# Square sums on GpSimd, norm operations among the residuals, and filter spectra dealt behind two channel tiles

## The chip, the cores and the metric

The kernel runs on one core of a Trainium2 chip. TensorE (PE) multiplies, VectorE (DVE) and ScalarE (ACT) work elementwise, GpSimd (POOL) is a third, slower elementwise engine that also issues some DMAs, and SyncE (SP) issues most of them. Each engine works through its own queue in order; semaphores tie them together. SBUF is the on-chip memory, PSUM the memory into which TensorE accumulates and from which VectorE and ScalarE read. The metric is the time of one execution in microseconds (us), here the median of the runs.

## The reference

A two-layer encoder on a sequence of 1024 vectors of 1024 features. Layer 0 mixes by attention, layer 1 by a Hyena operator; each is followed by a convolutional feed-forward network (FFN). What this case touches:

```python
x = x + g2 * conv_ffn(h, ffn_w_up[i], ffn_conv_w[i], ffn_conv_b[i], ffn_w_down[i])   # layer 0, end
h = rmsnorm(x, norm1_g[i]) * (1.0 + sc1) + sh1                                       # layer 1, start

def hyena_mixer(h, ...):
    u = dwconv3(h @ w_in, conv_w, conv_b)          # 1024 -> 3072 channels, 3-tap convolution in time
    v, x1, x2 = jnp.split(u, 3, axis=-1)
    ...                                            # filt: two filters from a small network
    kf = jnp.fft.rfft(k2, axis=0)                  # the filter spectra
    gates = (x1, x2)
    zc = v
    for o in range(HY_ORDER):
        zf = jnp.fft.rfft(zc.astype(jnp.float32), n=2 * L, axis=1)
        y = jnp.fft.irfft(zf * kf[None, :, o], n=2 * L, axis=1)[:, :L]
        zc = gates[o] * (y.astype(h.dtype) + skip[o] * zc)
    return zc @ w_out
```

The norm divides each time step by the root of the mean of its squares over all 1024 features, so no output of it exists before the last feature tile of `x` is done. The spectra of the filters do not depend on `x`.

## The kernel before

Activations lie feature-major: 8 tiles of 128 features x 1024 time steps, worked on in two halves of 512 time steps (`HS`). Every matrix product is made of three matmuls on operands that are split into a high and a low part: high x high, low x high, high x low. One matmul multiplies a 128x128 weight block by 128x512 of the activations.

**The seam.** The last part of layer 0's FFN (`ffn(0, ...)`, which calls `seam`, L241) runs in an order written out by hand for TensorE, VectorE and ScalarE. For each half, eight steps: TensorE accumulates a feature tile in `d_ps` (L1296); VectorE adds it to the residual stream (`xd`, `res`, L980); ScalarE squares the new `xd` (`sq`, L981); VectorE adds the square to the running sum `ssq` (L268; the first square is the sum's start and the last is left to TensorE). Then `rstd_sums` (L230, L231) sums `ssq` and the last square over the partitions by 16 tiny matmuls with a column of ones, ScalarE takes the root (L232), VectorE the reciprocal (L233), and `rstd_spread` (L237) puts it on all partitions in a PSUM tile called `nrm`. `norm_ops` (L306) then lists 16 operations of VectorE per half: a scale (L314, `tt<-xd,acol,nrm`) and a low part (L318, `fh_l<-tt,mod,fh_h`) for each of the eight feature tiles; the high part between them (L315, `fh_h`) is ScalarE's. The dictionary `plan` says how many of the first half's 16 operations are run behind each step of the second half; before, it is empty, and four (`MID`) are run behind the last step. The others run as the matmuls of the next stage need them.

**The opening of the Hyena layer.** `w_in` has 24 channel tiles of 128 channels, 48 matmuls of 128x512 each (24 per half). Channel tiles 0 and 1 start inside the seam with their first half (`w_in_half`, `gemm_h`, L358). Then `w_in_stream` (L1382) yields after every matmul, so that others can be put between: the second half of channel tiles 0 and 1, channel tile 2 with a PSUM buffer of its own (pool `y1`), and then the others with a ring of two PSUM buffers (`pst`, which tiles 0 and 1 also use). Behind each channel tile, `dwconv` convolves in time: ScalarE starts `u` from the PSUM tile (L363) and VectorE adds the two other taps (L364, L365); the PSUM buffer is free when the last of them is done. Four transposes each (`u_tr`, L1389) turn half of a `u` into time-major form, which ScalarE copies to `gs` (L1391). The tuple `TRM` and the pair (10, 22) say ahead of which matmul of a channel tile such a group stands.

**Filter spectra.** `Filt` (L542) has eight units. Each loads the time-domain filter (`eo<-ed`, L557, 1 MB for each of two parts); the first load waits for a copy from the last low parts of the norm into the buffer (L556). `dif` makes sums and differences on VectorE (`pm`, `u`, `t`, `hf`, `ge`, `ri`, L372, L375), and TensorE multiplies them by a table (`f_ps`, L578 and following). While the units run, `MM_RATE` deals matmuls of `w_in_stream` among them by an account of VectorE's and TensorE's time. `MM_PRE` is the number of matmuls drawn ahead of it; before, 1 + 0, where the one draw runs the whole opening up to the end of channel tile 2.

**The conv stage** multiplies the spectra and transforms back (`z_ps` L1551, `ab_ps` L1573, `prod` L1643); the matmuls of `w_in` that are left are dealt among its steps by `rate` (L1751).

Outside the blocks written out by hand a scheduler orders the instructions by priorities (`HP` raises one); in the blocks from the spectra on only TensorE's order is by hand.

## Time and profile before

| | |
|---|---|
| Three runs | 2951.65, 2956.84, 2960.39 us; median 2956.84 |
| Profiled execution | 2955.43 us, its span 2953.7, mean granted clock 0.986 |
| TensorE busy | 2820.9 us (96%) |
| VectorE busy | 2326.6 us (79%) |
| ScalarE busy | 1237.2 us (42%) |
| GpSimd busy | 324.6 us (11%) |
| Seam and opening | from about 1434.7 to 1515.8 us of the span |
| Filter spectra | 1515.8 to about 1815 |
| Conv stage with matmuls of `w_in` | about 1815 to 1994 |

Rows of a timeline give the start and the length in us, the engine, the line of the kernel, the operation, the tile written and those read, the shape, and how many like instructions are put together; in brackets stands how long the engine had been idle before, and what it had waited for. Rows of windows give for each stretch the busy time and number of instructions of each engine, TensorE's granted clock (1.00 is full), the busy share of the DMA engines, and GB/s. Rows of waits give the total, the number and the longest wait.

### The profile page before, as it was taken

Reading aid. Unit: us, or ns where it says so; the run is one execution under the profiler, and the core shown is the slowest. Engines: PE = TensorE matmul, PEld = TensorE weight load, DVE = VectorE, ACT = ScalarE, POOL = GpSimd, SP = SyncE. Lnnn points to the kernel's source line nnn. Section 1 sums busy time; section 2 is a strip of 40 time slices with the busy share of each in tenths; the row PEclk is TensorE's granted clock in tenths of the full one; section 3 lists DMA queues with packets and bytes.
Section 4 is the critical chain, followed back from the end, with each engine's and each line's share of the span. In section 5 each row is a group of like instructions: output and inputs, shape, how many; then the busy total and the mean of one; then the engine's idle time right before and its main releaser. Section 6 shows DMA issues by size and latency. Waiting matters only on the chain.

```text
span 2953.7 us, 36529 instructions
## 1 busy us (share of the span) xinstructions
PE 2820.9 (96%) x13152; PEld 2301.5 (78%) x13152; DVE 2326.6 (79%) x3221; ACT 1237.2 (42%) x2004; POOL 324.6 (11%) x356
## 2 busy tenths in 40 slices
PE   5989999999999999999999999999988999999998
PEld 4777777778888887888777877877767788887887
DVE  8787989869988887877767885888867887777544
ACT  3557888843544443343432332223233433333211
POOL 0064564400011001111000000000000000000000
PEclk9999999999999999999999999999999999999999
DMA  7262222145455555665455665555754332224321
GB/s 276 92 185 66 54 76 51 50 169 190 139 187 182 177 174 176 207 184 156 140 199 190 225 206 197 174 173 184 245 195 153 123 104 87 86 79 143 122 86 57
DMA packets 221400, 440.02 MB, mean 149 GB/s; under 512 B 22210, under 2 KB 117218, under 8 KB 216740
## 3 DMA queue, kind: packets, MB, share of 16 engines
q1 hardware_dynamic: 184292, 391.54, 39.7%
q0 software_dynamic: 36928, 46.15, 5.7%
q8 instruction: 104, 1.70, 0.2%
q14 instruction: 76, 0.62, 0.1%
HBM read 308.62 MB, written 128.99 MB: 148 GB/s over the span
## 4 chain that ended last, share of the span: by engine, by line
PE 63%; DVE 9%; DMA 4%; issue 1%; ACT 1%; SPq 0%; DVEq 0%; ACTq 0%; POOLq 0%
PE w_ps L1063 26%; PE d_ps L183 14%; PE u_ps L1437 5%; PE d_ps L1296 2%; PE wo_y L183 2%; PE ab_ps L1573 2%; PE f_ps L183 2%; PE g_ps L358 2%; PE f_ps L578 1%; PE v_ps L358 1%; PE f_ps L579 1%; DVE prod L1643 1%; PE wo_y L1036 1%; DMA y<-yd 1%; DMA rd<-fw 1%
## 5 line engine op out<-in xcount | busy, mean ns | idle before, releaser
L1155 ACT CAST w_hi<-u 128x1024 fp32r<-128x1024 f32 x120 | 125.8, 1049 | 234.6 <-PE w_ps L1063 221.9
L162 DVE TENSOR_TENSOR pT_lo<-pt_ps,pT_hi 128x512 fp32r<-128x512 f32 x256 | 167.8, 681 | 46.7 <-ACT pT_hi L859 44.9
L1261 DVE SCALAR_TENSOR_TENSOR xd<-d_ps,mod,xd 128x1024 f32<-128x1024 f32 x104 | 132.7, 1280 | 76.5 <-PE d_ps L183 76.4
L1063 PE MATMUL w_ps<-t_h,w_hi 128*128 128x512 f32 x480 | 190.6, 397 | 1.9 <-ACT w_hi L1155 1.9
L1063 PE MATMUL w_ps<-t_h,w_lo 128*128 128x512 f32 x480 | 189.9, 397 | 0.4 <-DVE w_lo L162 0.4
L1063 PE MATMUL w_ps<-t_l,w_hi 128*128 128x512 f32 x480 | 190.0, 396 | 0.0
L162 DVE TENSOR_TENSOR w_lo<-u,w_hi 128x1024 fp32r<-128x1024 f32 x120 | 146.6, 1223 | 54.4 <-ACT w_hi L1155 54.2
L859 ACT CAST pT_hi<-pt_ps 128x512 fp32r<-128x512 f32 x256 | 145.1, 588 | 69.5 <-PE pt_ps L854 63.7
L183 PE MATMUL d_ps<-s_hi,wd_lo 128*128 128x512 f32 x544 | 170.0, 391 | 0.0
L183 PE MATMUL d_ps<-s_lo,wd_hi 128*128 128x512 f32 x544 | 169.9, 391 | 0.0
L183 PE MATMUL d_ps<-s_hi,wd_hi 128*128 128x512 f32 x544 | 168.9, 390 | 0.0
L838 DVE TENSOR_REDUCE nmx<-s_ps 128x1 f32<-128x1024 f32 x128 | 155.5, 1217 | 12.8 <-PE s_ps L831 10.9
L854 PE MATMUL pt_ps<-ident,p_t 128*128 128x128 f32 x1024 | 154.4, 274 | 10.0 <-DVE pT_lo L162 9.0
L854 PEld LDWEIGHTS pt_ps<-ident,p_t 128*128 128x128 f32 x1024 | 126.5, 141 | 44.8 <-DVE pT_lo L162 8.0
L848 ACT ACTIVATE p_t<-s_ps,nmx 128x1024 f32<-128x1024 f32 x128 | 143.7, 1124 | 3.5 <-DVE nmx L838 2.3
L1437 PE MATMUL u_ps<-fh_h,w_lo 128*128 128x512 f32 x368 | 132.3, 418 | 2.4 <-DMA w_lo<-wld 2.4
L1573 PE MATMUL ab_ps<-prod,dfti 128*128 128x256 f32 x512 | 124.2, 386 | 7.7 <-DVE prod L1643 2.4
L1437 PE MATMUL u_ps<-fh_l,w_hi 128*128 128x512 f32 x368 | 127.5, 413 | 0.0
L1063 PE MATMUL w_ps<-fh_h,w_hi 128*128 128x512 f32 x320 | 124.9, 390 | 0.7 <-ACT w_hi L1155 0.7
L1063 PE MATMUL w_ps<-fh_l,w_hi 128*128 128x512 f32 x320 | 124.8, 390 | 0.0
L1063 PE MATMUL w_ps<-gh_h,w_hi 128*128 128x512 f32 x320 | 124.7, 390 | 0.0
L1063 PE MATMUL w_ps<-gh_l,w_hi 128*128 128x512 f32 x320 | 124.7, 390 | 0.0
(424 smaller groups left out, 7568.4 us busy)
## 6 DMA issues: line engine op xcount, KB each, us to landing
u<-in_w_up_dram SPq DMA_DIRECT2D x80, 512.0 KB
w_raw<-in_w_down_dram SPq DMA_DIRECT2D x44, 512.0 KB
sg<-gate SPq DMA_DIRECT2D x40, 512.0 KB
w_raw<-sg SPq DMA_DIRECT2D x40, 512.0 KB
w_raw<-in_ada_w_dram SPq DMA_DIRECT2D x32, 512.0 KB
ed<-eo SPq DMA_DIRECT2D x64, 256.0 KB
eo<-ed SPq DMA_DIRECT2D x16, 1024.0 KB
kd<-k_sb SPq DMA_DIRECT2D x64, 256.0 KB
```

The source lines that it names most:

```text
L162: V.tensor_tensor(lo, src, hi.bitcast(F32), op=SUB)
L183: mm(out[:, cs], lhsT=a, rhs=b[:, cs], start=start and i == 0, stop=stop and i == 2)
L358: mm(pp[:, HS[hf]], lhsT=(wh, wh, wl)[i][:, ks], rhs=hd[hf][i % 2][k], start=k == 0 and i == 0, stop=k == n - 1 and i == 2)
L838: V.tensor_reduce(nmx, s_t[u, i], op=ALU.max, axis=AX.X, negate=True)
L848: nc.scalar.activation(p_t, s_ps, AF.Exp, bias=nmx, accum_out=sums[u][:, i:i + 1])
L854: nc.tensor.transpose(tp[:, i * P:(i + 1) * P], pts[u, i][:, sb * P:(sb + 1) * P], ident)
L859: nc.scalar.copy(ph, pt_t[u, sb][0])
L1063: mm(out, lhsT=(w[0], w[0], w[1])[i][:, k * P:(k + 1) * P], rhs=b[i % 2][k], start=k == 0 and i == 0, stop=k == 3 and i == 2)
L1155: nc.scalar.copy(w[0], src)
L1261: ins = V.scalar_tensor_tensor(x[dt_], yp, gate[dt_], x[dt_], op0=MUL, op1=ADD)
L1437: mm(yp[:, HS[hf]], lhsT=(wh, wh, wl)[i][:, k * P:(k + 1) * P], rhs=hd[hf][i % 2][k], start=k == 0 and i == 0, stop=k == KT - 1 and i == 2)
L1573: mm(ap[:, i], lhsT=dfti[:, m, :], rhs=v, start=n == 0, stop=n == len(ops) - 1)
```

## The change

Two things change in the seam of layer 0, three in the opening. (1) `plan` is {3: 1, 4: 1, 5: 1, 6: 1}: one norm operation of the first half behind each of the steps 3 to 6 of the second. (2) The six adds of squares of the second half are GpSimd's. (3) The opening block holds channel tiles 0 and 1 alone; channel tile 2 is streamed like those behind it, takes its buffer from the ring of two, and the pool `y1` is gone. (4) `MM_PRE` is 60: 48 matmuls of the block and 12 of channel tile 2 are drawn in the hand order ahead of the first unit of the spectra, and the dealing begins there. (5) Channel tile 2 has transposes ahead of its matmuls 18, 26, 38 and 46 instead of 10, 22, 40 and 47. The number of matmuls in `rate` follows from it. The lines of the changed kernel lie by one higher in the seam.

```diff
@@ -26,11 +26,12 @@
 NFFT = 2 * L
 LAGS = 2
 TRM = (40, 47)
+TR2 = (18, 26, 38, 46)
 NZ = 10
 ZC = 0.3
 TC_DELAY = 4
 TC_SPACE = 0
-MM_PRE = 0
+MM_PRE = 60
 PP = 300
 EK = ((0, 7), (1, 3))
 TC0 = 3
@@ -238,7 +239,7 @@
 
     MID = 4
 
-    def seam(n, step, result, ops, tps, at, plan, nxt=(), lows=()):
+    def seam(n, step, result, ops, tps, at, plan, nxt=(), lows=(), adders=(V, V)):
         todo = []
 
         def run(k):
@@ -265,7 +266,7 @@
 
             def later():
                 if not first and i < n - 1:
-                    V.tensor_tensor(ssq[:, cs], ssq[:, cs], sq, op=ADD)
+                    adders[hf].tensor_tensor(ssq[:, cs], ssq[:, cs], sq, op=ADD)
             return later, sq
 
         with tc.manual_schedule(engines={mybir.EngineType.PE, mybir.EngineType.DVE, mybir.EngineType.Activation}):
@@ -1299,7 +1300,8 @@
         def result(hf, dt_):
             return res(yps[hf, dt_], x[dt_], gate[dt_], HS[hf], dt_ == 0, sq_tile(sqp))
 
-        seam(KT, step, result, lambda hf, yt: ops(hf, tp_, yt), tps, ((12, 20), at), plan, nxt() if nxt else ())
+        seam(KT, step, result, lambda hf, yt: ops(hf, tp_, yt), tps, ((12, 20), at), plan, nxt() if nxt else (),
+             adders=(V, V if l else nc.gpsimd))
         tail_end(tps, False)
         sqp.release()
         (sb if l else wdt).release()
@@ -1355,7 +1357,7 @@
             yield from gemm_h(w_in2, hd, True, range(1))
         return go()
 
-    ffn(0, "left", "right", pre, ops0, {}, (0, 6), w_in_half, l1_work)
+    ffn(0, "left", "right", pre, ops0, {3: 1, 4: 1, 5: 1, 6: 1}, (0, 6), w_in_half, l1_work)
 
 
     up = [tc.alloc_tile_pool(name="hy_u", bufs=1)]
@@ -1364,7 +1366,6 @@
     dftf = dftp.tile([P, NFW + 6, P], F32, name="dftf")
     nc.sync.dma_start(dftf, t["dft_f"])
     fpool = tc.alloc_tile_pool(name="flt", bufs=1, side="right")
-    y1 = tc.alloc_tile_pool(name="y1", bufs=1, space=PSUM)
     F = Filt(fpool, "f", dftf)
     units = [(o, c4) for c4 in range(4) for o in range(2)]
     vdifs, f_done, seen = [], [], set()
@@ -1380,7 +1381,7 @@
             yield c, 0
 
     def w_in_stream():
-        pend, gs, gbufs, first, nw = [], None, 2, [], 0
+        pend, gbufs, nw = [], 2, 2
 
         def channels_to_time(u, gs, ct, hf):
             part, c4 = ct // 8, ct % 8 // 2
@@ -1406,38 +1407,30 @@
                 dwconv(yp, [col(C_HW + 24 * i + c_) for i in range(3)], col(C_HB + c_), u)
             pend.extend(lambda hf=hf: channels_to_time(u, gs, c_, hf) for hf in range(2))
 
-        for ct in [2 * p_ + i for p_ in (0, 1, 2, 3, 4, 5, 8, 9, 6, 7, 10, 11) for i in range(2)]:
+        gs = new_gs()
+        for k in range(KT):
+            for (wh, wl), yp in w_in2:
+                for i in range(3):
+                    mm(yp[:, HS[1]], lhsT=(wh, wh, wl)[i][:, k * P:(k + 1) * P], rhs=hd[1][i % 2][k],
+                       start=k == 0 and i == 0, stop=k == KT - 1 and i == 2)
+                    yield
+        for c_ in range(2):
+            conv(c_, w_in2[c_][1], gs)
+        for ct in [2 * p_ + i for p_ in (1, 2, 3, 4, 5, 8, 9, 6, 7, 10, 11) for i in range(2)]:
             with tc.high_priority(HP):
                 nw += 1
-                if ct < 2:
-                    first.append(w_in2[ct])
-                    continue
                 if nw % 3 or f_done:
                     wh, wl = wt.load(t["w_in"][ct], wld[ct])
                 else:
                     wh, wl = load_split(t["w_in"][ct], fpool, 1, lo_src=wld[ct])
-            if ct < 3:
-                first.append(((wh, wl), y1.tile([P, L], F32, name="u_ps", tag="y")))
-                order = [(hf, k, c_, i) for hf, cs in ((1, (0, 1)), (0, (2,)), (1, (2,))) for k in range(KT)
-                         for c_ in cs for i in range(3)]
-            else:
-                yp = pst("u_ps")
-                order = [(hf, k, 3, i) for k in range(KT) for i in range(3) for hf in range(2)]
-            for m, (hf, k, c_, i) in enumerate(order):
-                if c_ < 3:
-                    (wh, wl), yp = first[c_]
-                    m -= 48
-                    if m == 0:
-                        for c_ in range(2):
-                            if c_ == 0:
-                                gs = new_gs()
-                            conv(c_, first[c_][1], gs)
-                if pend and m in (TRM if ct > 3 else (10, 22) + TRM):
+            yp = pst("u_ps")
+            order = [(hf, k, i) for k in range(KT) for i in range(3) for hf in range(2)]
+            for m, (hf, k, i) in enumerate(order):
+                if pend and m in (TRM if ct > 2 else TR2):
                     pend.pop(0)()
                 mm(yp[:, HS[hf]], lhsT=(wh, wh, wl)[i][:, k * P:(k + 1) * P], rhs=hd[hf][i % 2][k],
                    start=k == 0 and i == 0, stop=k == KT - 1 and i == 2)
-                if ct > 2:
-                    yield
+                yield
             if ct % 2 == 0:
                 if f_done and gbufs == 2:
                     up.pop().release()
@@ -1447,8 +1440,6 @@
                 assert len(vdifs) < 2
                 gs = new_gs()
             conv(ct, yp, gs)
-            if ct == 2:
-                yield
         for f in pend:
             for _ in range(FLUSH):
                 yield
@@ -1463,11 +1454,10 @@
             yield v
 
     gemm = counted(w_in_stream())
-    for _ in range(1 + MM_PRE):
-        next(gemm)
-    y1.release()
     F.ps = f_ps = tc.alloc_tile_pool(name="flt_ps", bufs=3, space=PSUM, side="right")
     with tc.manual_schedule(engines={mybir.EngineType.PE}):
+        for _ in range(MM_PRE):
+            next(gemm)
         owed = 0.0
         for dve, pe in F.run(units, vdifs):
             owed += (MM_RATE * dve - pe) / 0.16
@@ -1748,7 +1738,7 @@
     n_tc = n_wo = 0
     with tc.manual_schedule(engines={mybir.EngineType.PE}):
         w = sum(max(c - MM_CBASE, MM_CMIN) for n in range(G_END) for c in step_cost(n))
-        rate = (1 + 21 * 48 + 2 * FLUSH - n_mm[0]) / w
+        rate = (48 + 22 * 48 + 2 * FLUSH - n_mm[0]) / w
         for n, c in conv_steps(JOBS, on_done):
             if gemm:
                 owed += rate * max(c - MM_CBASE, MM_CMIN)
```

VectorE at the end of the seam, from the fifth residual of the second half to the reciprocal (`xd_1086n` is feature tile n of the residual stream, `fh_l` a low part, `tt` a scaled tile). Before:

```order
L980 SCALAR_TENSOR_TENSOR xd_10864<-d_ps,mod,xd_10864 128x512
L268 TENSOR_TENSOR ssq<-ssq,sq 128x512
L980 SCALAR_TENSOR_TENSOR xd_10865<-d_ps,mod,xd_10865 128x512
L268 TENSOR_TENSOR ssq<-ssq,sq 128x512
L980 SCALAR_TENSOR_TENSOR xd_10866<-d_ps,mod,xd_10866 128x512
L268 TENSOR_TENSOR ssq<-ssq,sq 128x512
L980 SCALAR_TENSOR_TENSOR xd_10867<-d_ps,mod,xd_10867 128x512
L268 TENSOR_TENSOR ssq<-ssq,sq 128x512
L314 SCALAR_TENSOR_TENSOR tt<-xd_10860,acol,nrm 128x512
L314 SCALAR_TENSOR_TENSOR tt<-xd_10861,acol,nrm 128x512
L314 SCALAR_TENSOR_TENSOR tt<-xd_10862,acol,nrm 128x512
L318 SCALAR_TENSOR_TENSOR fh_l_13380<-tt,mod,fh_h_13372 128x512
```

VectorE at the same place in the changed kernel:

```order
L315 SCALAR_TENSOR_TENSOR tt<-xd_10860,acol,nrm 128x512
L981 SCALAR_TENSOR_TENSOR xd_10864<-d_ps,mod,xd_10864 128x512
L315 SCALAR_TENSOR_TENSOR tt<-xd_10861,acol,nrm 128x512
L981 SCALAR_TENSOR_TENSOR xd_10865<-d_ps,mod,xd_10865 128x512
L315 SCALAR_TENSOR_TENSOR tt<-xd_10862,acol,nrm 128x512
L981 SCALAR_TENSOR_TENSOR xd_10866<-d_ps,mod,xd_10866 128x512
L319 SCALAR_TENSOR_TENSOR fh_l_13380<-tt,mod,fh_h_13372 128x512
L981 SCALAR_TENSOR_TENSOR xd_10867<-d_ps,mod,xd_10867 128x512
L315 SCALAR_TENSOR_TENSOR tt<-xd_10863,acol,nrm 128x512
L319 SCALAR_TENSOR_TENSOR fh_l_13381<-tt,mod,fh_h_13373 128x512
L315 SCALAR_TENSOR_TENSOR tt<-xd_10864,acol,nrm 128x512
L319 SCALAR_TENSOR_TENSOR fh_l_13382<-tt,mod,fh_h_13374 128x512
```

The adds are gone from VectorE; three scales and a low part stand between the residuals instead, and eight operations of the first half are ahead of the second half's reciprocal where four were.

VectorE behind the norm, from the last low part on (`pm`, the numbered `u` and `t`, `hf`, `ge` belong to the first spectra unit; `u<-u_ps,cols,u` are the taps of channel tiles 0 and 1). Before:

```order
L318 SCALAR_TENSOR_TENSOR fh_l_13406<-tt,mod,fh_h_13398 128x512
L556 COPY eo<-fh_l_13387 1x1
L556 COPY eo<-fh_l_13402 1x1
L364 SCALAR_TENSOR_TENSOR u<-u_ps,cols,u 128x1023
L372 TENSOR_TENSOR pm<-eo 128x1024
L372 TENSOR_TENSOR pm<-eo 128x768
L372 TENSOR_TENSOR pm<-eo 128x256
L364 SCALAR_TENSOR_TENSOR u<-u_ps,cols,u 128x1023
L365 SCALAR_TENSOR_TENSOR u<-u_ps,cols,u 128x1023
L372 TENSOR_TENSOR u_13951<-pm 128x256 x2
L372 TENSOR_TENSOR t_13949<-pm 128x2x256 x2
```

VectorE at the same place in the changed kernel, from the first `pm` on:

```order
L373 TENSOR_TENSOR pm<-eo 128x1024
L373 TENSOR_TENSOR pm<-eo 128x768
L373 TENSOR_TENSOR pm<-eo 128x256
L373 TENSOR_TENSOR u_13882<-pm 128x256 x2
L365 SCALAR_TENSOR_TENSOR u<-u_ps,cols,u 128x1023
L373 TENSOR_TENSOR t_13880<-pm 128x2x256 x2
L376 SCALAR_TENSOR_TENSOR hf<-pm 128x512
L376 SCALAR_TENSOR_TENSOR ge<-pm,eo 128x512 x2
L365 SCALAR_TENSOR_TENSOR u<-u_ps,cols,u 128x1023
L366 SCALAR_TENSOR_TENSOR u<-u_ps,cols,u 128x1023
```

The operations of the spectra now stand ahead of the taps; the last row, the second tap of channel tile 0, is the thirteenth instruction behind `eo`.

TensorE at the border between the two opening channel tiles and channel tile 2, with the semaphores of its waits (DMAHW and DMASW are loads). Before:

```order
L1437 MATMUL u_ps<-fh_l_13406,w_hi 128x512
L1437 MATMUL u_ps<-fh_h_13398,w_lo 128x512
L1437 MATMUL u_ps<-fh_h_13372,w_hi 128x512 [waits DMAHW3_49,DMAHW4_49,DMAHW2_49,DMAHW5_49,DMAHW1_49,DMAHW6_49,DMAHW0_49,DMAHW7_49,PE_49,Activation_49]
L1437 MATMUL u_ps<-fh_l_13380,w_hi 128x512
L1437 MATMUL u_ps<-fh_h_13372,w_lo 128x512 [waits DMASW2_49]
L1437 MATMUL u_ps<-fh_h_13373,w_hi 128x512
```

TensorE there in the changed kernel:

```order
L1414 MATMUL u_ps<-fh_l_13406,w_hi 128x512
L1414 MATMUL u_ps<-fh_h_13398,w_lo 128x512
L1431 MATMUL u_ps<-fh_h_13372,w_hi 128x512 [waits DMAHW3_49,DMAHW4_49,DMAHW2_49,DMAHW5_49,DMAHW1_49,DMAHW6_49,DMAHW0_49,DMAHW7_49,DVE_49,Activation_49]
L1431 MATMUL u_ps<-fh_h_13391,w_hi 128x512
L1431 MATMUL u_ps<-fh_l_13380,w_hi 128x512
L1431 MATMUL u_ps<-fh_l_13399,w_hi 128x512
L1431 MATMUL u_ps<-fh_h_13372,w_lo 128x512 [waits DMASW2_49]
```

The first matmul of channel tile 2 (on `fh_h_13372`) now waits for VectorE too: for the second tap of channel tile 0, whose buffer it takes. Over the whole of TensorE's order, 134 matmuls of `u_ps` stand ahead of the first of `f_ps` where 170 did (with 2 groups of `u_tr` instead of 6), 700 among the spectra in both, 40 between the spectra and `z_ps`, and 278 in the conv stage where 242 did.

## The prediction, made before the result was known

> **What bounds the kernel now.** I read first the busy shares, then the windows around the seam (end of the first FFN, norm, opening of the Hyena layer), then TensorE's and VectorE's timelines there.
>
> ```profile
> PE 2820.9 (96%) x13152; PEld 2301.5 (78%) x13152; DVE 2326.6 (79%) x3221; ACT 1237.2 (42%) x2004; POOL 324.6 (11%) x356
> ```
>
> TensorE sets the end: it is idle for 133 us of the span of 2953.7. A change can pay only where TensorE is idle or at a low clock. The windows (span, busy time of PE, PEld, DVE, ACT, POOL, granted clock, DMA share, GB/s):
>
> ```profile
> 1463.00:1476.80 13.80, 13.80 (x51) 11.17 (x51) 13.41 (x22) 7.32 (x11) 0.00 (x0) 0.78 0.13 54
> 1488.50:1491.00 2.50, 0.09 (x2) 0.03 (x1) 1.37 (x2) 2.19 (x2) 0.49 (x1) 1.00 1.03 416
> 1502.00:1515.80 13.80, 10.60 (x50) 8.34 (x49) 3.52 (x5) 5.46 (x8) 0.53 (x1) 0.88 0.36 117
> 1515.80:1815.00 299.20, 295.57 (x1359) 240.48 (x1358) 241.05 (x363) 88.89 (x137) 7.43 (x14) 1.00 0.58 192
> 1815.00:1994.00 179.00, 170.50 (x781) 143.44 (x780) 131.33 (x190) 50.35 (x106) 2.12 (x4) 0.99 0.60 195
> ```
>
> The seam and opening hold the losses: idle and a clock of 0.78 and 0.88. The spectra stage (1515.8 to 1815) is TensorE's own work, 295.6 of 299.2, so it keeps its length and only its start can move. The conv stage behind it has 8.5 us of idle. TensorE through the seam:
>
> ```profile
> 1460.55 0.50 PE L358 MATMUL u_ps<-fh_h,w_hi 128*128 128x512 f32 x1 [2.85 <-ACT fh_h L315]
> 1460.89 0.28 PE L230 MATMUL nrm<-ones,ssq 128*128 128x1 f32 x2
> ...
> 1477.05 0.62 PE L1437 MATMUL u_ps<-fh_h,w_hi 128*128 128x512 f32 x2
> ...
> 1488.17 0.39 PE L1437 MATMUL u_ps<-fh_l,w_hi 128*128 128x512 f32 x1
> 1490.98 0.50 PE L1437 MATMUL u_ps<-fh_h,w_lo 128*128 128x512 f32 x1 [2.41 <-DMA w_lo<-wld]
> ...
> 1509.65 0.74 PE L1389 MATMUL u_tr<-ident,u 128*128 128x128 f32 x4 [1.59 <-DVE u L365]
> 1510.04 1.20 PE L1437 MATMUL u_ps<-fh_h,w_lo 128*128 128x512 f32 x2
> ...
> 1513.54 0.63 PE L1437 MATMUL u_ps<-fh_h,w_hi 128*128 128x512 f32 x2
> ...
> 1515.83 0.59 PE L578 MATMUL f_ps<-u,dftf 128*128 128x256 f32 x2
> ```
>
> TensorE's queue is in order. Half 1 of the two opening channel tiles starts at 1477.05; 49 matmuls later it is 1488.17, 0.227 each, so its 48 end at about 1487.95. Then come channel tile 2, the transposes, and the first spectra matmul at **1515.83**. VectorE there:
>
> ```profile
> 1456.38 0.75 DVE L980 SCALAR_TENSOR_TENSOR xd<-d_ps,mod,xd 128x512 f32<-128x512 f32 x1
> 1457.04 0.68 DVE L268 TENSOR_TENSOR ssq<-ssq,sq 128x512 f32<-128x512 f32 x1
> 1457.73 0.75 DVE L980 SCALAR_TENSOR_TENSOR xd<-d_ps,mod,xd 128x512 f32<-128x512 f32 x1
> ...
> 1463.39 0.18 DVE L233 RECIPROCAL nsd<-nsd 128x4 f32<-128x4 f32 x1 [1.66 <-ACT nsd L232]
> ...
> 1479.97 2.07 DVE L318 SCALAR_TENSOR_TENSOR fh_l<-tt,mod,fh_h 128x512 fp32r<-128x512 f32 x3
> 1482.08 0.20 DVE L556 COPY eo<-fh_l 1x1 f32<-1x1 f32 x2
> 1489.63 1.28 DVE L364 SCALAR_TENSOR_TENSOR u<-u_ps,cols,u 128x1023 f32<-128x1023 f32 x1 [7.35 <-ACT u L363]
> 1490.83 2.42 DVE L372 TENSOR_TENSOR pm<-eo 128x1024 f32<-128x1024 f32 x3
> ...
> 1495.55 0.75 DVE L372 TENSOR_TENSOR u<-pm 128x256 f32<-128x256 f32 x2
> 1496.22 1.29 DVE L372 TENSOR_TENSOR t<-pm 128x512 f32<-128x512 f32 x2
> 1497.42 0.68 DVE L375 SCALAR_TENSOR_TENSOR hf<-pm 128x512 f32<-128x512 f32 x1
> 1498.03 1.28 DVE L375 SCALAR_TENSOR_TENSOR ge<-pm,eo 128x512 f32<-128x512 f32 x2
> ```
>
> The 32 norm operations run back to back from the reciprocal, 28 of them in 18.6 us (0.663 each), and end at 1482.04.
>
> **The seam part.** The change puts four of the first half's norm operations between the residuals (there VectorE loses six adds of 0.67, 4.0 us, and gains four operations of 0.663), and gives the adds to GpSimd, which has nothing in the window of the norm (0.00, x0). The trace has no 128x512 add on GpSimd. Its nearest rows, and what VectorE did beside one:
>
> ```profile
> L192 POOL TENSOR_TENSOR ssq<-ssq,w_raw 128x1024 f32<-128x1024 f32 x28 | 67.4, 2406 | 0.5
> L903 POOL TENSOR_TENSOR ol<-o_s,oh 128x256 fp32r<-128x256 f32 x32 | 23.7, 740 | 1.2
> ```
> ```profile
> 167.32 4.96 POOL L192 TENSOR_TENSOR ssq<-ssq,w_raw 128x1024 f32<-128x1024 f32 x2
> ...
> 289.97 2.39 POOL L192 TENSOR_TENSOR ssq<-ssq,w_raw 128x1024 f32<-128x1024 f32 x1
> ```
> ```profile
> 167.10 5.46 DVE L719 TENSOR_TENSOR qk_b<-qk_n,Tq 128x256 f32<-128x256 f32 x2
> ...
> 173.69 0.75 DVE L719 TENSOR_TENSOR qk_b<-qk_n,Tq 128x256 f32<-128x256 f32 x2
> ...
> 291.77 0.68 DVE L162 TENSOR_TENSOR pT_lo<-pt_ps,pT_hi 128x512 fp32r<-128x512 f32 x1
> ```
>
> Half of 2.41 is 1.20, twice 0.74 is 1.48; the shape is closer to the first, so 1.2, with 2.4 as the upper end and no gain below 0.67, VectorE's own price. Residuals come every 1.35 us (1456.38, 1457.73), so an add of 1.2 keeps up. But the pair of L719, both inputs in SBUF, took 5.46 beside GpSimd's two adds and 0.75 alone: VectorE stood still while GpSimd added. L162, with one of its inputs in PSUM, took no more than 0.68 inside GpSimd's add of 289.97. So the residuals and the scales (`nrm` lies in PSUM) pass, and a low part (`fh_l<-tt,mod,fh_h`) does not. [...]
>
> ```profile
> 1458.58 0.63 ACT L981 ACTIVATE sq<-xd 128x512 f32<-128x512 f32 x1 [0.73 <-DVE xd L980]
> ```
>
> One low stands among the residuals, ahead of the last: it waits for the fifth add (about 1457.7), so the last residual ends at 1459.1 instead of 1458.45, its square at 1459.8, the last add at 1459.6. The sums start near 1459.9, against 1460.89: 1.0 earlier. Behind the reciprocal stand 24 operations instead of 28, 2.65 us less. The norm ends **3.65 us earlier, near 1478.4**. Half 1 on TensorE then ends near 1485: 1.0 from the sums, and 1.7 if one slow window goes (a clock of 0.78 over 13.8 is 6.1 us at half clock, two windows).
>
> **The opening.** Its 96 matmuls of half 1 and channel tile 2 become 48 + 38 before the first spectra matmul, four groups of u_tr transposes go behind it, and channel tile 2 loses its own PSUM buffer. In the new order its first matmul waits for VectorE's last operation on `u` of channel tile 0 (buffer ring of two). On VectorE the first spectra's operations now stand ahead of that `u`, and these wait for `eo` from DRAM, issued behind the last norm operation. How long `eo` takes, by what SP's queue moved from 1482.3 to 1486.7 (packets, MB, share):
>
> ```profile
> q1 hardware_dynamic: 134, 1.05, 70.1%
> ```
>
> One `eo` is 1 MB and was issued first, so these are its bytes, and it lands 4.65 after the norm's end. Its lower bound is 2.5, 1.05 MB at the 416 GB/s of the window from 1488.5; its upper bound 8.9, as late as the `w_lo` that was issued beside it (1490.98). I take 4.65, the bytes seen: 1483.0. Then, at the distances from row to row: pm 2.34, u 0.67, the first L364 1.20 (1489.63 to 1490.83), t 1.20, hf 0.61, ge 1.20, the other L364 and the L365 1.20 each, together 9.6. **TensorE waits until 1492.6**, some 7.5 us, a new wait in the place of the 2.41 on `w_lo` (which lands 8.9 after the norm's end, 1487.3, and is hidden). Queued behind it are all 38 matmuls and the spectra.
>
> After an idle stretch TensorE is slow: from 1510.04 to 1513.54 eight matmuls took 3.50 instead of 1.82, 1.7 lost. I charge 1.7 once. [...]
>
> 38 x 0.227 = 8.6, two groups of transposes at 0.39 (1509.65 to 1510.04) = 0.8, and 1.7: first spectra at 1503.7, **12.1 earlier**. But 36 matmuls (8.2) and four groups (1.6) are still owed: the spectra stage deals 700 u_ps matmuls in both orders, the conv stage 278 instead of 242. Equal work gives 12.1 - 9.8 = 2.3. What the moved matmuls cost in the conv stage lies between 8.2 and nothing; its waits are
>
> ```profile
> PE z_ps L1551 <- DMA rix<-rd: 3.5, 1, 3.5
> PE ab_ps L1573 <- ACT ssq L1577: 2.0, 1, 2.0
> PE ab_ps L1573 <- ACT abx L1577: 2.0, 1, 2.0
> ```
>
> 7.5 us that 242 matmuls among them did not fill; a seventh more may fill a seventh of that, 1.1; I stay near the end that the standing waits speak for. **Sum: 3.4 us gained.** On the profiled execution (2955.43, of which 1.7 lie around its span) that is 2952.0, on the median shown, 2956.84, it is 2953.4. I say 2952.5.
>
> **Rivals.**
>
> *Faster: the moved matmuls fill the conv stage's holes.* They cost next to nothing there: 7.5 are hidden, the gain is 2.3 + 7.5 = 9.8, the time 2946. For it: 7.5 us of waits against 8.2 of matmuls. Against: the filler there was already plentiful and the waits stood.
>
> *Slower: the PSUM wait grows.* Were `eo` as late as `w_lo` (8.9 instead of 4.65), TensorE would wait until 1496.9 and have a second slow window: 4.25 + 1.7 more against 2.3, a loss of 3.6, 2960. It decides from `u` later than 1494.9 (2.3 behind 1492.6). For it: the weights are fetched at the same time; against it: `eo` was issued ahead and its bytes were through first.
>
> *GpSimd is late.* At 2.4 an add, six in a row from 1451.1 (the second residual and its square, six steps of 1.35 ahead) end at 1465.5, and the reciprocal near 1468 holds VectorE back; the 24 operations behind it end at 1484, 5.6 later than forecast, a loss of 3.3, 2960. Break-even is an add of about 1.85: six of it end at 1462.2, 2.3 behind 1459.9. [...]
>
> *The seam doesn't move the opening.* If `eo` were not released by the norm's end, the 3.65 would be lost, and 2.3 + 1.1 - 3.65 leaves nothing: 2956.5. The copies right behind the last low speak against it.
>
> **How the numbers follow.** Forecast 0.50, faster 0.28, longer PSUM wait 0.12, GpSimd 0.06, no shift 0.04. About 0.3% (8.9 us) is what a measurement can tell from no change; below 2948.0 is faster, above 2965.7 slower. Faster takes the first rival, 0.28, and 0.02 of the forecast. Each late case alone gives 2960; slower needs both, or one beyond its bound: 0.08 of their 0.18. The forecast's own range is 2949 to 2957; the first rival pulls the low end to 2944, the two late ones the high end to 2961.
>
> **What would show it.** Right: squares added on GpSimd at about 1.2 us; the last `fh_l` near 1478; a wait of 7 to 10 us of u_ps on VectorE's `u` right behind half 1, with slow clock behind it; no wait on `w_lo`; first f_ps near 1503.7; a spectra stage of the same length; a conv stage some 8 us longer. Wrong: no such wait, a first f_ps before 1498 or after 1508, or a conv stage as long as before.

## The result

The changed kernel takes **2971.82 us** (median of five runs, 2968.94 to 2975.48) against 2956.84 before: 1.0055 times, 95% interval 1.004 to 1.007. It is 15 us slower, and 2971.82 lies outside the predicted range of 2944 to 2961. Its profiled execution has a span of 2973.7, against 2953.7; it is the slowest of the five, so the differences between the two profiles (20.0 us) are larger than the one between the medians. The engines' busy times in the profile after:

```profile
PE 2829.6 (95%) x13152; PEld 2308.1 (78%) x13152; DVE 2323.1 (78%) x3215; ACT 1237.3 (42%) x2004; POOL 333.8 (11%) x362
```

TensorE has the same 13152 matmuls and is busy for 8.7 us longer, at a mean granted clock of 0.980 instead of 0.986. Its idle time grew by 11.3 us more. Where, the windows after show (span, busy time of PE, PEld, DVE, ACT, POOL, granted clock, DMA share, GB/s): the spectra stage, from there to the first `z_ps`, and the conv stage up to the first transposition of its result in two pieces.

```profile
1507.90:1817.00 309.10, 299.62 (x1367) 243.53 (x1366) 241.32 (x363) 90.99 (x140) 7.96 (x15) 0.99 0.57 189
1817.00:1829.70 12.70, 10.02 (x49) 7.93 (x47) 2.57 (x2) 3.26 (x5) 0.00 (x0) 0.97 0.41 123
1829.70:2009.70 180.00, 174.62 (x791) 147.11 (x792) 132.58 (x192) 50.50 (x104) 2.12 (x4) 0.97 0.60 191
2009.70:2046.20 36.50, 30.33 (x129) 24.67 (x128) 26.62 (x39) 11.74 (x26) 1.06 (x2) 0.91 0.59 194
```

The same stretches before:

```profile
1815.00:1824.20 9.20, 9.20 (x44) 7.58 (x43) 0.00 (x0) 1.48 (x3) 0.00 (x0) 1.00 0.68 217
1824.20:1993.60 169.40, 160.90 (x736) 135.51 (x735) 130.93 (x190) 48.48 (x102) 2.12 (x4) 0.99 0.60 193
1993.60:2025.40 31.80, 31.01 (x145) 25.98 (x143) 28.11 (x40) 12.78 (x29) 1.06 (x2) 1.00 0.78 259
```

In the table the first column counts from the start of the FFN's tail steps (1432.56 before, 1434.30 after) to the first spectra matmul. The other stages end at the last spectra matmul, the first `z_ps` and the first `z_tr`; the last column is the sum, up to that `z_tr`. Behind it the two kernels differ by less than 1 us.

| us | to the spectra | spectra | gap | conv stage | sum |
|---|---|---|---|---|---|
| before | 83.3 | 299.0 | 9.4 | 201.2 | 592.9 |
| after | 73.6 | 309.0 | 12.8 | 216.5 | 611.9 |
| difference | -9.7 | +10.0 | +3.4 | +15.3 | +19.0 |

So the spectra did start earlier, but the stages from there on took 28.7 us more. Some of that belongs to this one execution: three runs below that deal the same 700 matmuls among the spectra (`e2_open`, `e5_gap76`, `e8_nw1`) have a spectra stage of 307.6, 306.7 and 305.6.

**The seam went as worked out.** GpSimd's adds in the groups after, and VectorE's rows at the end of the seam and behind the norm:

```profile
L269 POOL TENSOR_TENSOR ssq<-ssq,sq 128x512 f32<-128x512 f32 x6 | 8.1, 1346 | 54.8 <-ACT sq L982 54.4
```
```profile
1457.43 0.74 DVE L315 SCALAR_TENSOR_TENSOR tt<-xd,acol,nrm 128x512 f32<-128x512 f32 x1
1458.13 0.75 DVE L981 SCALAR_TENSOR_TENSOR xd<-d_ps,mod,xd 128x512 f32<-128x512 f32 x1
1458.79 1.61 DVE L319 SCALAR_TENSOR_TENSOR fh_l<-tt,mod,fh_h 128x512 fp32r<-128x512 f32 x1
1460.33 0.74 DVE L981 SCALAR_TENSOR_TENSOR xd<-d_ps,mod,xd 128x512 f32<-128x512 f32 x1
...
1480.03 0.20 DVE L557 COPY eo<-fh_l 1x1 f32<-1x1 f32 x2
1485.24 2.43 DVE L373 TENSOR_TENSOR pm<-eo 128x1024 f32<-128x1024 f32 x3 [5.01 <-DMA eo<-ed]
...
1494.03 1.27 DVE L366 SCALAR_TENSOR_TENSOR u<-u_ps,cols,u 128x1023 f32<-128x1023 f32 x1
```

The low part among the adds took 1.61 instead of 0.75 and held back the last residual; the scales kept 0.74. The norm ends 45.7 behind the tail's start instead of 49.5.

**The wait for the PSUM buffer is there.** TensorE after:

```profile
1486.92 0.39 PE L1414 MATMUL u_ps<-fh_h,w_lo 128*128 128x512 f32 x1
1495.40 1.19 PE L1431 MATMUL u_ps<-fh_h,w_hi 128*128 128x512 f32 x2 [8.09 <-issue]
...
1507.90 0.60 PE L579 MATMUL f_ps<-u,dftf 128*128 128x256 f32 x2
...
1829.69 1.19 PE L1541 MATMUL z_ps<-rix,dftf 128*128 128x256 f32 x2 [2.68 <-issue]
...
1835.68 1.22 PE L1541 MATMUL z_ps<-rix,dftf 128*128 128x256 f32 x2 [2.23 <-DMA rix<-rd]
...
2018.59 1.09 PE L1390 MATMUL u_tr<-ident,u 128*128 128x128 f32 x4 [5.42 <-DVE u L366]
```

The second tap of channel tile 0 ends at 1495.3, and the matmul starts at 1495.40, after 8.09 of idle (the trace names no releaser there, the ends agree). The last three rows are waits further on. The prediction had one of their kind in its rows, the 3.5 on `rix` before; the 2.68 and the 5.42 are new.

### The profile page after: what moved, and what is told of

It reads as the page before. It is cut to its first block, busy times and chain, and to the rows that moved or that the text cites. A ratio compares the mean times of both kernels' runs of the same rounds, so it can differ in the third digit from the quotient of the medians.

```text
span 2973.7 us, 36537 instructions
## 1 busy us (share of the span) xinstructions
PE 2829.6 (95%) x13152; PEld 2308.1 (78%) x13152; DVE 2323.1 (78%) x3215; ACT 1237.3 (42%) x2004; POOL 333.8 (11%) x362
## 4 chain that ended last, share of the span: by engine, by line
PE 65%; DVE 7%; DMA 4%; issue 1%; ACT 1%; SPq 0%; POOL 0%; DVEq 0%; ACTq 0%; POOLq 0%
PE w_ps L1064 26%; PE d_ps L184 14%; PE u_ps L1431 6%; PE ab_ps L1563 2%; PE wo_y L184 2%; PE f_ps L184 2%; PE g_ps L359 1%; PE d_ps L1297 1%; PE v_ps L359 1%; PE f_ps L579 1%; PE f_ps L580 1%; PE wo_y L1037 1%; DVE prod L1633 1%; DMA y<-yd 1%; PE z_ps L1541 1%
## 5 line engine op out<-in xcount | busy, mean ns | idle before, releaser
L839 DVE TENSOR_REDUCE nmx<-s_ps 128x1 f32<-128x1024 f32 x128 | 155.6, 1217 | 10.8 <-PE s_ps L832 8.9
L1431 PE MATMUL u_ps<-fh_h,w_hi 128*128 128x512 f32 x352 | 120.9, 417 | 8.1 <-issue 8.1
L1064 PE MATMUL w_ps<-gh_h,w_lo 128*128 128x512 f32 x320 | 124.6, 389 | 0.0
```

Source lines behind the costliest of these rows:

```text
L839: V.tensor_reduce(nmx, s_t[u, i], op=ALU.max, axis=AX.X, negate=True)
L1064: mm(out, lhsT=(w[0], w[0], w[1])[i][:, k * P:(k + 1) * P], rhs=b[i % 2][k], start=k == 0 and i == 0, stop=k == 3 and i == 2)
L1431: mm(yp[:, HS[hf]], lhsT=(wh, wh, wl)[i][:, k * P:(k + 1) * P], rhs=hd[hf][i % 2][k], start=k == 0 and i == 0, stop=k == KT - 1 and i == 2)
```

## The experiments

Times are medians beside runs of the kernel before in the same series (2955.4 to 2956.5); stages come from one trace of each run, cut as in the table above.

### Which part costs

`e1_seam` is the kernel before with the seam part alone, `e2_open` the changed kernel without it.

```diff
 e1_seam, on the kernel before:
-                    V.tensor_tensor(ssq[:, cs], ssq[:, cs], sq, op=ADD)
+                    adders[hf].tensor_tensor(ssq[:, cs], ssq[:, cs], sq, op=ADD)
-    ffn(0, "left", "right", pre, ops0, {}, (0, 6), w_in_half, l1_work)
+    ffn(0, "left", "right", pre, ops0, {3: 1, 4: 1, 5: 1, 6: 1}, (0, 6), w_in_half, l1_work)
 e2_open, on the changed kernel:
-             adders=(V, V if l else nc.gpsimd))
+             adders=(V, V))
-    ffn(0, "left", "right", pre, ops0, {3: 1, 4: 1, 5: 1, 6: 1}, (0, 6), w_in_half, l1_work)
+    ffn(0, "left", "right", pre, ops0, {}, (0, 6), w_in_half, l1_work)
```

> The seam part alone: four norm operations among the residuals and the six adds on GpSimd, the opening of the Hyena layer as before (channel tile 2 with its own PSUM buffer, all of it ahead of the spectra). Theory (all of the loss comes from the opening part): the last fh_l of the norm ends 3.5 us earlier against the start of the FFN's tail, first f_ps some 3 us earlier, the spectra stage stays at 299 us and the conv stage at 201 us (z_ps to z_tr), time about 3 us below before, 2953 to 2955. Rival (GpSimd's adds and its lock on VectorE cost): norm no earlier, or stages behind it longer, 2960 or more.

Measured: 2952.35 us, 0.9987 (0.9977 to 0.9996), a little below what was expected. Norm 45.9, spectra at 76.9, spectra stage 299.0, conv stage 197.8.

> The opening part alone: spectra dealt behind two channel tiles, no buffer of its own for channel tile 2, the seam as before (adds on VectorE, no norm operation among the residuals). Theory: the whole loss is here, and the seam's gain is missing: spectra stage some 309 us, conv stage some 216 us, time 2973 to 2977, some 3 us above the changed kernel. Rival (seam part costs): nearer to before, 2955 to 2963.

Measured: 2971.71 us, 1.006 (1.0044 to 1.0076): spectra at 75.0, spectra stage 307.6, gap 13.0, conv stage 216.0.

The seam part alone gains 4 us (1 to 7 by the interval) and lengthens nothing. The opening part alone costs the whole loss. It was a miss that `e2_open` is no slower than the changed kernel: the seam's gain does not come through there. The rows of VectorE show why the spectra start only 1.4 us earlier with the seam part (73.6 against 75.0). In `e2_open` the first tap stands ahead of `pm`, and the wait is 7.4 us; in the changed kernel the norm ends 5.4 earlier, all of the first spectra operations go ahead of the tap, and the tap that frees the buffer ends only 2.6 earlier (61.0 instead of 63.6 behind the tail's start), with 10.2 us of slow clock (granted 0.50) behind the wait instead of 6.8.

In `e1_seam` these operations stand ahead of the taps as well (`pm` at 1484.57, second tap at 1493.44), yet TensorE runs straight into channel tile 2:

```profile
1486.09 0.39 PE L1438 MATMUL u_ps<-fh_l,w_hi 128*128 128x512 f32 x1
1486.32 0.40 PE L1438 MATMUL u_ps<-fh_h,w_lo 128*128 128x512 f32 x1
1486.55 0.40 PE L1438 MATMUL u_ps<-fh_h,w_hi 128*128 128x512 f32 x1
```

It has its own buffer. The order on VectorE and the ring of two together make the wait; with the ring and another order half of it is left (`e6_gate`, below).

### Is it that the stream of `w_in` is behind?

The changed kernel starts the spectra with 36 fewer matmuls of `w_in` done and deals the same 700 among them, so it is 36 behind at their end. Three runs take that lag away in different places: `MM_PRE` is the number drawn ahead, `MM_RATE` the pace among the spectra, `MM_GAP` the number between the spectra and the first `z_ps`.

```diff
 e3_pre96, on the changed kernel:
-MM_PRE = 60
+MM_PRE = 96
 e7_rate113, on the changed kernel:
-MM_RATE = 1.1
+MM_RATE = 1.13
 e5_gap76, on the changed kernel:
-MM_GAP = 40
+MM_GAP = 76
```

> The changed kernel with MM_PRE 96 instead of 60: all of channel tile 2 ahead of the first unit of the spectra, so that 170 u_ps matmuls stand in the opening, 700 among the spectra and 242 in the conv stage, as in the kernel before; the wait for the PSUM buffer stays. Theory A (what costs downstream is the stream of w_in being 36 matmuls behind when the spectra end): spectra stage 300 us, from its end to the first z_ps 9 us instead of 13, conv stage 201 us, first f_ps about 1515 against before's 1516; time 2955 to 2959. Theory B (the order that the scheduler gives VectorE and SP in the spectra stage, from the early start or from the two-buffer ring, costs by itself): spectra stage stays near 309 us, time 2964 to 2970.

Measured: 2954.22 us, 0.9997 (0.9986 to 1.0009), a little below the range. Spectra at 82.9, spectra stage 299.9, gap 9.4, conv stage 201.0.

> The changed kernel with MM_RATE 1.13 instead of 1.1, so that 737 matmuls of w_in are dealt among the spectra (135 ahead, 39 between, 241 in the conv stage): the early start stays, but the stream is no longer behind when the spectra end. Theory A (being 36 behind at the end of the spectra is what costs in the gap and the conv stage): gap 9.4 and conv stage 201 us as before, spectra stage 299 + 8.4 + 0.7 = 308 if its stalls go too, 316 if they stay; time 2953 to 2955, or 2960 to 2963 with the stalls. Rival (the early start itself costs): conv stage stays above 210, time 2970 or more.

Measured: 2953.28 us, 0.9991 (0.998 to 1.0002). Spectra at 74.7, spectra stage 309.5 with 37 more matmuls in it (8.4, so 301 without them), gap 9.2, conv stage 198.8.

> The changed kernel with MM_GAP 76 instead of 40: 36 matmuls of the conv stage moved to between the last f_ps and the first z_ps. Theory A: the matmuls whose weights lie in the spectra's pool are then done when the conv stage loads into that space, so that z_ps waits for nothing (2.7 and 2.2 us and the slow windows behind them gone), third pool there from the start; gap 17.5 us, conv stage 201 us, together 219 instead of 229: time about 2962. Rival (the conv stage is long by work alone or by its own order): no gain, 2970 to 2973.

Measured: 2960.1 us, 1.001 (1.0 to 1.0021). Spectra stage 306.7, gap 18.6, conv stage 200.1; these two are 218.7 against 229.3 in the changed kernel and 210.6 before: here the 36 matmuls cost their own 8.2 and no more.

All three give theory A right. With the stream caught up, whether ahead of the spectra or among them, 17.6 and 18.5 us of the changed kernel's time are gone; caught up in the gap, 11.7. The early start itself cost nothing: `e7_rate113` keeps it. It also gained nothing clear: the intervals of `e3_pre96` and `e7_rate113` both take in the time of the kernel before. The wait of 8.1 us is still there in both.

### What the lag does: three places

**The gap.** The first loads of the conv stage on SP's queue, after and before:

```profile
1824.75 0.36 SPq L1516 DMA_DIRECT2D kt<-kd  x1
```
```profile
1817.72 0.36 SPq L1526 DMA_DIRECT2D kt<-kd  x1
```

They go out 7.9 us behind the last spectra matmul (1816.9) instead of 2.9 (1814.8). The conv stage's tiles lie where the spectra's pool lay, and every third channel tile of `w_in` has its weights in that pool. In the changed kernel such a tile is under way when the spectra end, 18 of its 48 matmuls done. `e8_nw1` shifts which tiles these are.

```diff
 e8_nw1, on the changed kernel:
-        pend, gbufs, nw = [], 2, 2
+        pend, gbufs, nw = [], 2, 1
```

> The changed kernel with the count that chooses which weight tiles lie in the spectra's own pool begun one lower (every third channel tile, now 3, 6, 9, ... instead of 2, 5, 8, ...): 700 among the spectra as in the changed kernel, 29 between them and z_ps, 289 in the conv stage. Theory A: the channel tile that is under way when the spectra end no longer has its weights in that pool, so the conv stage's loads of kt and rix go out within 3 us of the last f_ps instead of 7.8, and z_ps does not wait for them; gap 7 us instead of 12.8, slow windows there 3.4 us instead of 10.2; together some 6 us below the changed kernel, 2964 to 2967. Rival (the loads wait for something else): gap 10 us or more with the wait on rix in it, time as the changed kernel's.

Measured: 2965.13 us, 1.0039 (1.0026 to 1.0052). The first `kt` goes out at 1813.68, 3.0 behind the last spectra matmul (1810.73); gap 8.2 instead of 12.8, and from the gap to the first `z_tr` 6.8 us of slow windows (granted clock 0.50) instead of 17.1. The loads waited for those weights. A wait of 2.6 on `rix` is left and the gap is 1.2 longer than expected, so "does not wait" was too much. Gap and conv stage together are 6.2 shorter than in the changed kernel, as expected, with 223.1; the spectra stage, 305.6, is shorter too, which the edit does not explain.

**The spectra stage.** Its waits after, before, and in `e9_eob4`, which has a fourth buffer for `eo`:

```profile
PE f_ps L579 <- DVE ri L376: 5.3, 3, 2.8
PE u_tr L1390 <- DVE u L366: 4.0, 3, 1.9
```
```profile
PE u_tr L1389 <- DVE u L365: 2.1, 2, 1.9
PE f_ps L578 <- DVE ri L375: 1.3, 2, 1.1
```
```profile
PE u_tr L1390 <- DVE u L366: 2.9, 3, 1.9
PE f_ps L579 <- DVE ri L376: 1.4, 2, 1.1
```

VectorE after, at the longest of these waits:

```profile
1729.43 0.69 DVE L376 SCALAR_TENSOR_TENSOR ri<-hf,ge 128x512 f32<-128x512 f32 x1 [0.94 <-PE f_ps L580]
1733.07 0.41 DVE L563 TENSOR_TENSOR eo<-eo,srow 1x256 f32<-1x256 f32 x1 [2.94 <-DMA eo<-ed]
...
1736.47 0.68 DVE L376 SCALAR_TENSOR_TENSOR ri<-hf,ge 128x512 f32<-128x512 f32 x1
```

A tiny add on one partition belongs to a later job, and waits in VectorE's queue for that job's `eo`, issued at 1724.20; the `ri` for which TensorE waits stands behind it, and behind 3.1 us of `hf` and `pm`, the latter the next job's. Each of the two longest waits of `f_ps` in this trace (2.75 and 2.30) is followed by one slow window (from 1736.9 and 1771.0, 3.41 us each at a granted clock of 0.50).

```diff
 e9_eob4, on the changed kernel:
-EOB = 3
+EOB = 4
-EK = ((0, 7), (1, 3))
+EK = ((0, 7), (1, 3), (1, 3))
```

> The changed kernel with four buffers for eo instead of three, so that each load of eo stands one job earlier. Theory C (the spectra stage is longer because VectorE's add of srow waits for an eo that was issued late, 2.9 and 2.7 us, and f_ps then for ri with a slow window each): these waits go, spectra stage 309 to about 302, time 2964 to 2966. Rival (the stage is longer by the order of u and the transposes, or by TensorE's work): it stays above 306, time 2969 or more.

Measured: 2965.54 us, 1.0034 (1.0022 to 1.0046); spectra stage 301.1, no slow window in it. With the fourth buffer 7.9 of the 10.0 us are gone; against the 305.6 to 307.6 of the other three runs it is 4.5 to 6.5, and the medians differ by 6.3. Gap and conv stage are as in the changed kernel, 13.2 and 216.9. What went are TensorE's waits for `ri`. VectorE's own waits for `eo` did not, against the expectation:

```profile
1718.14 0.41 DVE L563 TENSOR_TENSOR eo<-eo,srow 1x256 f32<-1x256 f32 x1 [5.38 <-DMA eo<-ed]
1718.48 0.67 DVE L376 SCALAR_TENSOR_TENSOR ri<-hf,ge 128x512 f32<-128x512 f32 x1
```

TensorE had other matmuls to run meanwhile. Before, such a wait of 3.20 stood on VectorE at 1705.39, and TensorE's longest wait for `ri` was 1.1. So in these traces a late `eo` costs only where TensorE already waits for an `ri` behind it. That the buffer helps is shown; whether by the earlier loads or by another order on VectorE is not.

**The conv stage.** Of its 15.3 us more, the 36 matmuls are 8.2 and a group of transposes 0.4. Idle time grew by 2.2 (9.3 to 11.5, from the windows). The rest, 4.5, agrees with the slow clock: between the first `z_ps` and the first `z_tr` lie 16.4 us of slow windows, 12.4 of them with work in them, against 3.4 before, and work in them took about twice its time (two rows of `z_ps` are 0.86 us apart at 1830.67, 0.43 at 1839.97). They stand behind the two waits for the loads, and behind the wait of 5.42 at 2018.59. There the last channel tile's transposes are due at step 30 of the stage (a step is a group of `z_ps` and `ab_ps`, and a later job needs these channels), one step behind that tile's last matmul; before, two steps lay between. From TensorE's order one sees also that 26 matmuls are forced at step 5, since the third pool of the conv stage is opened only when a further channel tile is finished, and that steps 6 to 8 then have none; before, these steps have 12, 6 and 3. What the burst at step 5 and the late transposes cost by themselves was not tried.

### The wait for the buffer by itself

`e6_gate` is `e3_pre96` with the first loads of `eo` held back until `u` of channel tile 0 is done, so that the taps stand ahead of the spectra's operations.

```diff
 e6_gate, on e3_pre96:
-            es = [self.load(*j, after=hd[h_][1][k].bitcast(F32)[0:1, 0:1]) for j, (h_, k) in zip(jobs, EK[:EOB - 1])]
+            es = [self.load(*j, after=us[0][0:1, 0:1]) for j in jobs[:EOB - 1]]
```

> The kernel of e3_pre96 (170 / 700 / 40 / 242 u_ps matmuls by stage), with the first two loads of eo held back until u of channel tile 0 is done instead of until the norm's low parts are, so that VectorE convolves channel tiles 0 and 1 ahead of the first spectra operations. Theory (the wait of 8.1 us for the PSUM buffer is there because pm and what follows it stand ahead of the second tap, and the slow clock behind it is a follow of that wait): wait about 4 us (ACT 1.1 and two taps 2.4 behind half 1), first f_ps 6 us earlier than in e3_pre96 (some 77 after the FFN tail's start against 82.9), other stages unchanged; time 2947 to 2950. Rival (eo later by 8 us starves the first spectra): the first f_ps no earlier or the spectra stage longer by what is gained, 2954 or more.

Measured: 2952.98 us, 0.9994 (0.9983 to 1.0006). The wait in its trace, and that of `e3_pre96`:

```profile
PE u_ps L1432 <- ACT u L364: 4.0, 1, 4.0
```
```profile
PE u_ps L1431 <- issue: 8.1, 1, 8.1
```

The wait is halved as worked out, and one slow window of 3.4 stands behind it instead of 10.2. The spectra start 3.1 earlier (79.8 against 82.9), not the 6 expected, with the norm 0.6 later and one slow window more at the seam (6.8 us against 3.4). `eo` is used 18 us later than in the changed kernel (69.0 behind the tail's start against 50.9), and the first spectra do not wait for it. The medians of the two differ by 1.2 us, less than these runs can tell apart, and 2952.98 lies above the 2947 to 2950 that were expected.

### The two halves of the seam part

```diff
 e11_adds, on the kernel before: the adders as in e1_seam, plan stays {}
 e12_plan, on the kernel before: the plan as in e1_seam, adds stay on VectorE
```

> The kernel before with the six adds of squares of the second half on GpSimd, and nothing else (no norm operation among the residuals). Theory (a low part beside GpSimd's add is what delayed the last residual, by 0.65 us; the adds themselves keep up): no fh_l stands among the adds, so the sums start 0.6 us earlier than in e1_seam, near 27.0 us behind the FFN tail's start, against 28.3 before; 28 operations stay behind the reciprocal, so the last fh_l ends near 47.9, against 45.9 in e1_seam and 49.5 before; time 1 to 2 us below before. Rival (GpSimd's reads slow VectorE's residuals or scales): sums no earlier than 28.

Measured: 2954.59 us, 1.0003 (0.9993 to 1.0013). GpSimd's adds are done at 1458.1, but the sums start at 1459.1, 2.6 behind the last FFN matmul (3.2 before, 2.3 in `e1_seam`), and the norm ends at 50.7 instead of the expected 47.9.

> The kernel before with four norm operations among the residuals and the adds left on VectorE. Theory (VectorE has no room among the residuals, 1.34 of 1.36 us a step, so the operations only gain where the adds are gone): each of the four puts the residuals back by 0.66, sums near 30.9 us behind the FFN tail's start against 28.3, the last fh_l near 49.5 as before; time as before, 2954 to 2959. Rival (there is room, and the gain is the plan's alone): last fh_l near 47, time as e1_seam's, 2952.

Measured: 2956.04 us, 1.0001 (0.9992 to 1.001). The last residual is put back to 28.4 behind the tail's start from 25.9, the sums to 29.0 (30.9 had been expected), and the norm ends at 49.0.

Neither half shows a gain in time alone, though their intervals touch that of `e1_seam`. The traces are clearer. From the start of the last FFN matmul to the norm's end it is 24.7 us before, 23.8 with the adds, 24.0 with the plan, and 21.1 with both. Without the plan, the first matmul of `w_in`, which stands ahead of the sums in TensorE's queue, waits for the first high part, and the scales that it needs come behind the residuals; the expectation of 27.0 for the sums had forgotten that:

```profile
1458.76 0.50 PE L358 MATMUL u_ps<-fh_h,w_hi 128*128 128x512 f32 x1 [2.25 <-ACT fh_h L315]
1459.10 0.28 PE L230 MATMUL nrm<-ones,ssq 128*128 128x1 f32 x2
```

Without the adds on GpSimd, VectorE has no room among the residuals.

### A version that beats both kernels

`e14_manual_tr` is `e1_seam` with the opening in TensorE's hand order and the transposes placed where VectorE's taps were done.

```diff
 e14_manual_tr, on e1_seam:
-                if pend and m in (TRM if ct > 3 else (10, 22) + TRM):
+                if pend and m in {2: (42, 46), 3: (10, 16, 36, 46)}.get(ct, TRM):
-    for _ in range(1 + MM_PRE):
-        next(gemm)
+    with tc.manual_schedule(engines={mybir.EngineType.PE}):
+        for _ in range(1 + MM_PRE):
+            next(gemm)
```

> The kernel of e1_seam (seam part, channel tile 2 with its own PSUM buffer and ahead of the spectra) with the opening in TensorE's hand order and the transposes of the first u where VectorE has them ready: matmuls 42 and 46 of channel tile 2 and 10, 16, 36, 46 of channel tile 3. Theory (no PSUM wait, no stream behind, and no waits at the transposes): first f_ps near 73 us behind the FFN tail's start against 76.9, with two groups of u_tr more among the spectra (0.8), other stages as in e1_seam; time 2948 to 2951, below both kernels. Rival (a transposition still waits for u and brings slow clock): no better than e1_seam, 2952 or more.

Measured: 2946.29 us, **0.9968** (0.996 to 0.9977), 9.7 us below the kernel before, 25 below the changed one, and a little below what was expected. Spectra at 73.3, spectra stage 299.8, gap 9.4, conv stage 197.9. The window from the last FFN matmul to the first spectra matmul in this kernel:

```profile
1461.00:1509.20 48.20, 45.44 (x208) 36.67 (x208) 36.92 (x54) 19.93 (x27) 4.54 (x6) 0.96 0.60 222
```

It reaches the spectra as early as the changed kernel does (73.6), with 170 matmuls of `w_in` done instead of 134. Which of its two parts, the hand order or the places of the transposes, brings the 6 us against `e1_seam` was not tried.

## Why the prediction was wrong

**The seam part: right.** An add of 1.20 on GpSimd was taken; it took 1.29 to 1.30 beside residuals and scales, and the one that began beside a low part 1.60. That a low part is held up beside an add, and scales and residuals are not, is what the rows show: 1.61 instead of 0.75, against 0.74 and 0.75. Norm 3.65 earlier was worked out, 3.8 measured.

**The wait for the PSUM buffer: right in cause, 7.5 worked out, 8.09 measured.** `pm` began 5.2 behind the norm's end instead of 4.65, and the tap ended 61.0 behind the tail's start where 60.0 was worked out (1492.6 less 1432.6).

**The slow clock behind it: mis-sized.** 1.7 was charged for one window; the slow stretch was 10.24 us at a granted clock of 0.50, of which 6 fell on work, 3.0 lost. The rival of a longer wait added 1.7 for a second slow window; no run shows that term, and what the changed kernel's trace shows behind the wait is the 10.24 us. In `e5_gap76` a slow stretch also followed on 3.42 us of which TensorE was busy for 1.49 (last section). The first spectra matmul came 9.7 us earlier against the tail's start, not 12.1: about 1.0 of it by the later tap, 1.3 by the clock.

**"It keeps its length and only its start can move": this is the first step that failed.** It was read from TensorE's busy share before, 295.6 of 299.2. That share holds for the order before. With the stream shifted against the jobs, VectorE's queue met a late `eo`, TensorE waited for `ri` behind it, and the stage grew by 10.0 us in the profiled execution. A fourth buffer for `eo` takes 7.9 of them away (`e9_eob4`); 0.8 are two groups of transposes that the prediction itself had counted as still owed.

**"Lies between 8.2 and nothing": the second step, and the larger.** The moved matmuls were costed as filler that at worst takes its own time. Gap and conv stage grew by 18.7, where 7.1 and 0.8 for two groups of transposes were charged. The bound left out what waits for that work to be finished. For the space of the weights this is shown (gap, `e8_nw1`); for the third pool and the last transposes that a conv job needs it is read from the order and the rows, without a run for each. `e5_gap76`, which does the same matmuls ahead of the conv stage, has that stage at 200.1 again. The three terms together, 2.4 in the opening, 9.2 in the spectra and 10.8 behind them, are the 22.4 us between the 3.4 gained that were forecast and the 19.0 lost in the table.

**The rivals.** Two came out slower. GpSimd being late needed adds of 1.85; they took 1.29 to 1.60. The other put the loss on the PSUM wait, and decided at 1494.9 on the scale before. The tap ended at 1495.3 in an execution that began its tail 1.7 later, which is 1493.6: it did not reach that point. The loss came from none of the rivals. "The seam doesn't move the opening" was nearer than its 0.04, as `e2_open` shows, but by the order on VectorE and not by `eo`. Faster by filled holes did not come: the two waits of 2.0 on ScalarE are gone from the conv stage, but 5.42 for the last transposes came in, and its idle time grew.

## What to carry to other kernels

Work that is moved behind a stage is not filler alone: ask what is released when it ends (space, a pool, an input of a later job), and cost the lag at each such place, not only the moved instructions. A stage that is 99% busy in one order need not be so in another; look for instructions in an in-order queue that belong to a later job, wait for a load, and stand ahead of something that another engine needs now. Give an early start only together with the pace that keeps the stream where it was: here one number (`MM_RATE`, 1.1 to 1.13) was worth 18 us by the medians.

## What the runs showed of the hardware

In the changed kernel's rows a scale and a residual, which have one input in PSUM, kept 0.74 and 0.75 us beside GpSimd's adds of 1.29 to 1.30; a low part, with both inputs in SBUF, took 1.61 instead of 0.75 (1.77 in `e1_seam`), and the add that began beside it 1.60.

How long TensorE waited did not by itself tell whether its clock fell. Between 1440 and 2060 us of the changed kernel's trace the stretches at a granted clock of 0.50 last 3.41 us or two or three times that (1736.90 to 1740.31, 2016.79 to 2023.62, 1491.14 to 1501.38); the starts at 1736.90 and 1771.03 are ten such steps apart. In `e5_gap76` a wait of 1.93 us lay within one step and the next ran at half clock; a wait of 2.2, spread over two, brought none. The two pairs of steps (busy time and clock as in the windows above):

```profile
1729.18:1732.60 3.42, 1.49 (x7) 1.01 (x6) 3.40 (x6) 0.58 (x1) 0.00 (x0) 1.00 0.39 131
1732.60:1736.01 3.41, 3.41 (x9) 2.66 (x9) 3.41 (x7) 0.01 (x1) 0.00 (x0) 0.50 0.06 20
1763.32:1766.73 3.41, 1.73 (x9) 1.49 (x9) 3.41 (x8) 0.21 (x1) 0.00 (x0) 1.00 0.46 154
1766.73:1770.14 3.41, 3.41 (x19) 2.82 (x18) 3.41 (x6) 1.18 (x2) 0.00 (x0) 1.00 0.23 77
```

Nor did the busy time within the step tell it alone. Here 1.49 of 3.42 us stood ahead of a slow step and 1.73 ahead of a full one; but in the changed kernel 1.57 stood ahead of a full one (from 1545.75) and 2.24 of 3.41 ahead of a slow one (from 1460.42), and in the kernel before 1.67 ahead of a slow one (from 1458.81). What decides was not shown.

After the 8.09 us of waiting in the changed kernel the granted clock was 0.50 for 10.24 us, though TensorE worked again for the last 6 of them: the slow step in which it began again (1494.55 to 1497.97, 75% busy) was followed by another. In the conv stage the clock behind the waits cost, by the sum above, an estimated 4.5 us, twice the 2.2 that the idle time itself added.
